# Serving the expert group with four passes fourth instead of third in the last layer of a decoder trunk

## The chip, the core and the metric

The kernel runs on one core of a Trainium2 chip. The metric is the device time of one execution in microseconds (us), lower is better. Five engines work side by side and wait for one another by semaphores: PE (matrix products, with PEld for its weight loads), DVE (vector), ACT (scalar), POOL (not used in the part treated here) and SP, which here only issues the DMAs that bring weights from the device memory (HBM) into the on-chip memory.

## What is computed

The reference is a decoder trunk of two layers over 256 tokens of width 1024. Each layer is a mixer of four kinds of attention heads, a cross-attention into 256 memory tokens, and a mixture of experts; each of the three is followed by a residual sum and a layer norm. The change concerns the order of work in the mixture of experts of the second (last) layer:

```python
def one_sequence(xs):
    g_logits = (xs @ w_group + b_group)
    g_idx = argmax(g_logits)                       # one group of 8 for each token
    g_weight = take_along_axis(softmax(g_logits), g_idx)
    e_logits = (xs @ w_expert + b_expert).reshape(s, 8, 4)[arange(s), g_idx]
    top_val, top_idx = top_k(e_logits, 2)          # two experts of 4 in that group
    top_w = softmax(top_val) * g_weight
    ...
    hid = silu(xs @ w_gate[e]) * (xs @ w_up[e])    # 1024 -> 256, twice
    return sum over e of (hid * gates[:, e]) @ w_down[e]   # 256 -> 1024
```

Each of the 32 experts has three matrices of 1 MB (gate, up, down), so a group of four experts has twelve tiles of 1 MB. How many tokens an expert gets is known only when the router has run.

## The kernel before, in words

The mixture of experts is the function `moe`. It serves the eight groups one after the other in the order of the table `SERVED[l]`: in the last layer 1, 3, 0, 2, 4, 5, 6, 7. For one group, the function `expert` runs a pass over up to 32 tokens of each of the four experts at once: the four experts take a quarter of PE's columns each. A pass is made of

- `up_to` with the four gate tiles (64 matmuls, L1277), a silu on ACT, then `up_to` with the four up tiles (64 matmuls, L1277); between the two stand the last four matmuls (L1322) of the previous group, put off as `late_back`;
- the gather of the next group's tokens (`gather_half`, 32 matmuls, L1227), and the transposition of the hidden values (`turned`, L1290);
- a branch (`over`, L1368) that is taken into further passes when an expert of the group has more than 32 tokens, more than 64 and so on, and that otherwise jumps over their code, which stands in the program behind it;
- the down product (`down`: 32 matmuls at L1306, then L1322 back to token order), with `begin` for the next group on DVE in between.

A light group has one pass. With these inputs, group 2 has a second pass, run whole before its own down product, and group 0 has three further passes. Group 0 stands in the table `SPREAD`: its three further passes run their first halves (`part`, function `hidden`) one behind the other, and their down halves (`rest`) afterwards, so that its gate and up tiles are given back between the two.

The weights come through a plan, one list of tiles in the order in which they are served. `feed` gives the next tile of the list a buffer as soon as one is free, and `done` frees a tile's buffer: the eight gate and up tiles of a group behind its branch (`free(g, 0, 8)`), its four down tiles behind its down product (`free(g, 8, 12)`). There are 21 such buffers in the last layer (six called main, nine ext, two in M, and R, VM, KT and xx), so a tile is loaded into the buffer of the tile 21 places ahead of it in the list. The loads are issued by SP in the order of the list, save that some small ones of the last group go early. The first 21 tiles of the last layer are loaded before its router has run, whether needed or not (L270); the rest are issued when the counts are known, each inside `tc.If`, so that an expert without tokens costs no load (L275). Two experts of group 6 have no tokens.

The up and down tiles of group 7 are loaded in pieces of 512 KB and 256 KB, and its down product runs over 512 columns first and then twice over 256, so that little is left to do when the last piece has landed.

Of the kernel before, what the change touches and what calls it, by code (L numbers as in the profile page):

```python
# [30 lines left out]
KEYS = 4  # L31


SERVED = [(0, 1, 2, 3, 4, 5, 6, 7), (1, 3, 0, 2, 4, 5, 6, 7)]
SPREAD = [(), (0,)]
TELL = [(3, 6), (3, 8)]


FIRST = [o[0] for o in SERVED]
GNUM = [[f if g == 0 else 0 if g == f else g for g in range(8)] for f in FIRST]  # L40
# [130 lines left out]
def trunk(ctx, tc, a, out, dbg=None, depth=DEPTH):  # L171
# [10 lines left out]
    def one(pool, name, shape, dt=F32):  # L182
        return tiles(pool, name, 1, shape, dt)[0]
# [27 lines left out]
    def square(l, m, q):  # L211
        wsq_i[l][m][q] = item(a["wsq"][l, m, q])
# [11 lines left out]
    for l in range(depth):  # L224
# [5 lines left out]
        for m in (3, 4):  # L230
            for q in range(4):
                square(l, m, q)
        for g, h in [(g, h) for g in SERVED[l + 1 == depth] for h in range(3)]:
            ids = exp_i[l].setdefault(g, {})
# [859 lines left out]
    def moe(l, pz, pb):  # L1094
# [3 lines left out]
        ff = one(pz, "ff", [128, 2, D])  # L1098
        served, spread = SERVED[late], SPREAD[late]
        follow = dict(zip(served, served[1:]))  # L1100
# [507 lines left out]
```

## Time and profile before

| | |
|---|---|
| median of 3 runs | 1008.36 us (1008.21 to 1008.63) |
| profiled execution | 1013.67 us, of which the span of the profile is 1011.9 us |
| busy: PE, PEld, DVE, ACT | 923.1, 688.2, 503.3, 340.9 us |
| DMA | 272.59 MB, mean 269 GB/s |

The span runs from the first to the last profiled instruction of the program. In the rows further below, a window is a stretch of the span (from:to) and its length in us, then the busy time and the count of PE, PEld, DVE, ACT and POOL, the clock granted to PE (1.00 is its higher level of 2.4 GHz, 0.50 its lower one of 1.2 GHz), the mean busy share of the DMA engines and the GB/s that they moved; a window of one line has only the engines that run it. A row of a timeline has the start, the duration, engine, line, operation, the tiles written and read, the count, and in brackets the idle time ahead of it with what ended that. A row that stands for several instructions has the duration of the whole run of them. Busy time is a mean over stages of different kinds: the mixture of experts of the last layer fills the last quarter of the span, from 757.81 us on, and only its stages matter for this change.

### The profile page before, as it was taken

What the parts mean: (1) busy time and instruction counts of PE and PEld (TensorE: products, weight loads), DVE (VectorE), ACT (ScalarE), POOL (GpSimd) and SP (SyncE); (2) the same over time, 40 slices, a digit from 0 to 9 for tenths busy, and PEclk for the clock granted to TensorE, in tenths of its full rate; (3) what the DMA queues carried; (4) which work ended last, traced back from release to release, by engine and by line L of the source; (5) the groups of instructions that cost most, each with busy time, mean ns of one, the idle gap of its engine ahead of it and who ended that gap; (6) DMA issues with size and microseconds to landing.
All of it is one profiled execution on the core that took longest, in us unless ns stands there. A gap on an engine that the chain in (4) does not pass through costs nothing. (4 is left out here: it accounts for less than half of the span.)

```text
span 1011.9 us, 19936 instructions
## 1 busy us (share of the span) xinstructions
PE 923.1 (91%) x7948; PEld 688.2 (68%) x7948; DVE 503.3 (50%) x1258; ACT 340.9 (34%) x736; POOL 0.2 (0%) x4
## 2 busy tenths in 40 slices
PE   7899999999998688989899999999999888997885
PEld 7888987898754354856368899789885564444541
DVE  5755755544653333323466575554465414644434
ACT  5454855343411121011144475435442121121111
POOL 0000000000000000000000000000000000000000
PEclk9999999999999899999999999999999999999998
DMA  9842334538769988999786244553784994719995
GB/s 351 343 147 99 134 128 161 209 125 331 293 268 422 424 348 367 424 425 420 250 336 229 108 147 180 174 208 110 288 351 196 421 387 183 318 58 421 422 363 203
DMA packets 43774, 272.59 MB, mean 269 GB/s; under 512 B 4832, under 2 KB 5344, under 8 KB 13280
## 3 DMA queue, kind: packets, MB, share of 16 engines
q1 hardware_dynamic: 43472, 270.26, 68.2%
q8 instruction: 86, 1.41, 0.5%
q14 instruction: 72, 0.59, 0.2%
q10 hardware_dynamic: 144, 0.33, 0.1%
HBM read 269.52 MB, written 1.05 MB: 267 GB/s over the span
## 5 line engine op out<-in xcount | busy, mean ns | idle before, releaser
L432 DVE SCALAR_TENSOR_TENSOR wl<-main,wh 128x1024 fp32r<-128x1024 f32 (+1 forms) x93 | 112.2, 1211 | 112.1 <-ACT wh L431 111.9
L431 ACT ACTIVATE wh<-main 128x1024 fp32r<-128x1024 f32 (+1 forms) x93 | 97.3, 1052 | 116.5 <-PE bank L438 68.3
L437 PE MATMUL bank<-xh,wh 128*128 128x256 f32 x368 | 108.8, 298 | 5.6 <-ACT xh L488 3.6
L438 PE MATMUL bank<-xl,wh 128*128 128x256 f32 x368 | 105.8, 288 | 1.0 <-DVE xl L432 0.6
L439 PE MATMUL bank<-xh,wl 128*128 128x256 f32 x368 | 104.9, 286 | 0.0
L1277 PE MATMUL bank<-ext,xg 128*32 128x256 f32 x912 | 88.2, 392 | 2.9 <-DMA ext<-exp 2.8
L1327 DVE TENSOR_TENSOR ff<-ff,bank 128x512 f32<-128x512 f32 x84 | 53.2, 681 | 49.9 <-PE bank L1322 49.9
L437 PEld LDWEIGHTS bank<-xh,wh 128*128 128x128 f32 x368 | 71.1, 194 | 7.0 <-ACT xh L488 4.1
L438 PEld LDWEIGHTS bank<-xl,wh 128*128 128x128 f32 x368 | 71.3, 194 | 2.2 <-DVE xl L432 0.9
L439 PEld LDWEIGHTS bank<-xh,wl 128*128 128x128 f32 x368 | 71.4, 194 | 0.1
L1277 PE MATMUL bank<-main,xg 128*32 128x256 f32 x640 | 66.1, 384 | 2.4 <-DMA main<-exp 2.4
L460 ACT ACTIVATE xg<-bank,prmb 128x128 f32<-128x128 f32 x64 | 24.0, 456 | 123.3 <-PE bank L1227 117.2
L1310 ACT ACTIVATE y<-bank,sm 128x512 fp32r<-128x512 f32 (+1 forms) x46 | 30.7, 669 | 103.5 <-PE bank L1306 76.1
L1322 PE MATMUL bank<-y,dt 128*128 128x512 f32 (+1 forms) x184 | 56.9, 422 | 7.9 <-DVE y L1311 7.2
L1306 PE MATMUL bank<-ext,dn 128*32 128x512 f32 (+1 forms) x212 | 46.6, 670 | 17.5 <-PEq L1368 6.8
L437 PE MATMUL bank<-wh,oh 128*128 128x512 f32 (+1 forms) x160 | 60.9, 380 | 0.0
L439 PE MATMUL bank<-wh,ol 128*128 128x512 f32 (+1 forms) x160 | 59.1, 369 | 0.0
L1322 PEld LDWEIGHTS bank<-y,dt 128*128 128x128 f32 x184 | 29.6, 188 | 43.2 <-ACT y L1310 16.4
L438 PE MATMUL bank<-wl,oh 128*128 128x512 f32 (+1 forms) x160 | 59.0, 369 | 0.0
L1277 PEld LDWEIGHTS bank<-ext,xg 128*32 128x32 f32 x912 | 42.6, 112 | 22.5 <-issue 4.7
L1227 PEld LDWEIGHTS bank<-dn,xhat 128*128 128x128 f32 x448 | 51.1, 192 | 5.8 <-issue 4.9
L1227 PE MATMUL bank<-dn,xhat 128*128 128x128 f32 x448 | 53.7, 278 | 0.0
(300 smaller groups left out, 2008.7 us busy)
## 6 DMA issues: line engine op xcount, KB each, us to landing
ext<-exp SPq DMA_DIRECT2D x75, 1024.0 KB, 16.6
main<-exp SPq DMA_DIRECT2D x54, 1024.0 KB, 12.8
main<-wsq SPq DMA_DIRECT2D x33, 1024.0 KB, 5.0
main<-win SPq DMA_DIRECT2D x22, 1024.0 KB, 6.8
M<-exp SPq DMA_DIRECT2D x17, 1024.0 KB, 15.0
VM<-exp SPq DMA_DIRECT2D x8, 1024.0 KB, 17.1
xx<-exp SPq DMA_DIRECT2D x7, 1024.0 KB, 14.0
M<-wsq SPq DMA_DIRECT2D x5, 1024.0 KB, 7.1
```

The lines of the kernel that those rows point to most:

```text
L431: ACT.activation(hi, src, AF.Copy, scale=scale)
L432: DVE.scalar_tensor_tensor(lo, src, scale, hi.bitcast(F32), op0=ALU.mult, op1=ALU.subtract)
L437: PE.matmul(psum, lh, rh, start=first, stop=False, skip_group_check=True)
L438: PE.matmul(psum, lh, rl, start=False, stop=False, skip_group_check=True)
L439: PE.matmul(psum, ll, rh, start=False, stop=last, skip_group_check=True)
L460: ACT.activation(dst, src, AF.Identity, bias=b, scale=g)
L1227: PE.matmul(b[:, k * 128:(k + 1) * 128], xhat[:, t, c:c + 128], d[:, t], start=(t == 0 and k == 0), stop=(t == 1), skip_group_check=True)
L1277: PE.matmul(pg[m * i:m * i + m, which * S:(which + 1) * S], x[:, k, m * i:m * i + m], w[:, k], start=(k == 0), stop=(k == 7), skip_group_c ...
L1306: PE.matmul(b[m * i:m * i + m], ht[:, f * 128 + m * i:f * 128 + m * i + m], w[:, o:o + n], start=(f == 0), stop=(f == 1), skip_group_check ...
L1310: ACT.activation(hi, b, AF.Copy, scale=gate)
L1322: PE.matmul(bs[t], dt[:, t * 128:(t + 1) * 128], y[i], start=(i == 0 and not held), stop=(i == 1), skip_group_check=bool(held))
L1327: DVE.tensor_add(o, o, bs[t])
```

## The change

One line of the table changes. In the last layer the order of the groups was 1, 3, 0, 2, 4, 5, 6, 7 and becomes 1, 3, 4, 0, 5, 2, 6, 7: group 4 is served before group 0, and group 5 before group 2. The plan of loads is built from the same table, so the weights of group 4 are also loaded ahead of those of group 0, and those of group 5 ahead of those of group 2. No instruction is added or removed.

```diff
-SERVED = [(0, 1, 2, 3, 4, 5, 6, 7), (1, 3, 0, 2, 4, 5, 6, 7)]
+SERVED = [(0, 1, 2, 3, 4, 5, 6, 7), (1, 3, 4, 0, 5, 2, 6, 7)]
 SPREAD = [(), (0,)]
 TELL = [(3, 6), (3, 8)]
```

On PE, behind the first pass of the third group served, the kernel before goes on with group 0 (spread over `part`):

```order
L1227 MATMUL bank_7_68<-dn_0_13924,xhat_0_77 128x128 x8
L1290 MATMUL bank_1_62<-cst_0_70,hs_0_13922 128x128 x2
L1368 COMPARE_AND_BRANCH
L1363 REGISTER_ALU
L1604 BRANCH_PREFETCH_HINT
L1227 MATMUL bank_3_64<-f_61_0_13925,xhat_0_77 128x128 x8
L1227 MATMUL bank_5_66<-f_61_0_13925,xhat_0_77 128x128 x8
```

At the same place the changed kernel stands in group 4, and what follows the branch is the code of a second pass that its 18 tokens of the fullest expert do not need:

```order
L1227 MATMUL bank_7_68<-dn_0_13924,xhat_0_77 128x128 x8
L1290 MATMUL bank_1_62<-cst_0_70,hs_0_13922 128x128 x2
L1368 COMPARE_AND_BRANCH
L1227 MATMUL bank_3_64<-f_61_0_13925,xhat_0_77 128x128 x8
L1227 MATMUL bank_5_66<-f_61_0_13925,xhat_0_77 128x128 x8
```

The tiles, the banks and the place of the branch are the same; the group behind them is another. What stood there moves one group down: from the row at which the fifth group reads its count (row 11751 on PE) the two programs are alike row by row again, with group 5 in the changed kernel where group 4 was.

On SP the loads stand in the same order, buffer by buffer. Only the branches between them move. Before, the three-way branch of group 0's `rest` stood behind the twelfth load that follows group 0's first branch, ahead of the one into VM:

```order
L275 DMA R_0_76<-exp 128x2048
L274 UNCONDITIONAL_BRANCH x2
L1368 COMPARE_AND_BRANCH x3
L1368 UNCONDITIONAL_BRANCH x4
L274 COMPARE_AND_BRANCH
L275 DMA VM_0_75<-exp 128x2048
```

Now it stands twelve loads later, ahead of the one into main_1:

```order
L275 DMA main_5_125<-exp 128x2048
L274 UNCONDITIONAL_BRANCH x2
L1368 COMPARE_AND_BRANCH x3
L1368 UNCONDITIONAL_BRANCH x4
L274 COMPARE_AND_BRANCH
L275 DMA main_1_121<-exp 128x2048
```

So the twelve loads from VM on, which before had to wait for a buffer of group 0's down tiles or of group 2, now take the buffers of group 4's down tiles and of group 0's gate and up tiles.

## Rows read from the trace of the kernel before

**Rows 1.** The page: the span, and the chain that ended last, by engine.

```profile
span 1011.9 us, 19936 instructions
DMA 8%; DVE 1%; PE 1%; issue 0%; SPq 0%; DVEq 0%; ACT 0%
```

**Rows 2.** Windows from group to group, served 1, 3, 0, 2, 4, 5, 6, 7.

```profile
757.81:776.46 18.65, 16.94 (x207) 10.23 (x207) 12.73 (x58) 5.80 (x14) 0.00 (x0) 1.00 0.26 92
776.46:797.52 21.06, 17.41 (x204) 9.98 (x203) 8.63 (x26) 3.43 (x8) 0.00 (x0) 1.00 1.01 421
797.52:874.16 76.64, 69.22 (x809) 40.56 (x808) 32.40 (x92) 14.47 (x32) 0.00 (x0) 1.00 0.74 306
874.16:911.19 37.03, 34.59 (x406) 20.14 (x405) 16.39 (x46) 7.18 (x16) 0.00 (x0) 1.00 0.40 154
911.19:936.18 24.99, 19.78 (x204) 10.73 (x203) 9.95 (x30) 3.54 (x8) 0.00 (x0) 0.93 1.01 422
936.18:956.27 20.09, 17.33 (x204) 9.98 (x203) 8.52 (x26) 3.53 (x8) 0.00 (x0) 1.00 1.01 422
956.27:976.41 20.14, 17.34 (x204) 9.98 (x203) 9.03 (x26) 3.53 (x8) 0.00 (x0) 1.00 1.01 413
976.41:1001.38 24.97, 22.29 (x199) 9.60 (x198) 6.97 (x13) 3.69 (x6) 0.00 (x0) 1.00 0.80 283
```

**Rows 3.** Windows in which the weight stream pauses (columns as in rows 2).

```profile
834.20:847.60 13.40, 11.35 (x168) 7.60 (x160) 2.88 (x10) 1.89 (x5) 0.00 (x0) 1.00 0.01 3
886.50:905.50 19.00, 17.28 (x203) 9.77 (x201) 5.28 (x15) 5.29 (x13) 0.00 (x0) 1.00 0.01 2
```

**Rows 4.** The last group: two windows, and a PE row with its wait.

```profile
976.41:988.83 12.42, 11.48 (x133) 5.11 (x132) 2.44 (x4) 1.67 (x2) 0.00 (x0) 1.00 0.86 285
990.33:994.82 4.49, 3.99 (x16) 0.72 (x16) 0.00 (x0) 0.00 (x0) 0.00 (x0) 1.00 1.04 392
...
991.79 0.62 PE L1306 MATMUL bank<-R,dn 128*32 128x512 f32 x1 [0.34 <-DMA R<-exp]
```

**Rows 5.** Timeline of PE: a light group's second pass; windows of L1306: its down product.

```profile
781.18 3.66 PE L1277 MATMUL bank<-ext,xg 128*32 128x256 f32 x64
...
950.19:953.84 3.65, 3.64 (x32) 0.94 (x32) 1.00 1.01 415
```

**Rows 6.** Timeline of group 4's branch: PE, then PEld.

```profile
927.69 1.62 PE L1306 MATMUL bank<-ext,dn 128*32 128x512 f32 x5 [4.15 <-DMA main<-exp]
...
933.21 0.16 PEld L1306 LDWEIGHTS bank<-ext,dn 128*32 128x32 f32 x8 [2.15 <-issue]
```

**Rows 7.** Timeline of SP from the first load that waits for the counts.

```profile
771.09 3.75 SPq L275 DMA_DIRECT2D main<-exp  x6
...
789.93 15.31 SPq L275 DMA_DIRECT2D ext<-exp  x7
807.37 0.33 SPq L275 DMA_DIRECT2D xx<-exp  x1
809.79 2.77 SPq L275 DMA_DIRECT2D main<-exp  x2
```

**Rows 8.** DMA issues at 802.47 and at 812.23 alone: size, us to landing.

```profile
ext<-exp SPq DMA_DIRECT2D x1, 1024.0 KB, 19.4
main<-exp SPq DMA_DIRECT2D x1, 1024.0 KB, 19.5
```

**Rows 9.** Timeline of PE: the last tile of the third group's second pass.

```profile
802.44 0.40 PE L1277 MATMUL bank<-R,xg 128*32 128x256 f32 x1
```

**Rows 10.** Windows of PE's idle stretch in group 4, and of what followed.

```profile
923.60:927.60 4.00, 0.00 (x0) 0.00 (x0) 0.04 (x1) 1.54 (x5) 0.00 (x0) 1.00 1.01 416
928.00:931.30 3.30, 3.30 (x18) 1.03 (x12) 1.94 (x11) 0.09 (x1) 0.00 (x0) 0.50 1.01 420
```

**Rows 11.** Timeline of PE: the end of group 5.

```profile
955.61 0.73 PE L1322 MATMUL bank<-y,dt 128*128 128x512 f32 x2 [1.11 <-DVE y L1311]
```

**Rows 12.** The page: the queue that brings instructions.

```profile
q8 instruction: 86, 1.41, 0.5%
```

## The prediction

> **What bounds the kernel now.** I looked first at the chain that ended last: of the span of 1011.9 us DMA holds 8% and no other wait over 1% [rows 1], so PE's work is the bound, with the weight stream breaking in at places. Second, windows from group to group, for the places [rows 2]. A light group with no wait takes 20.1 us; group 4 takes 24.99 and group 7 24.97. In the same view the stream is full (421 GB/s, 1.01 of the DMA engines) under groups 3, 4, 5 and 6, and not full under groups 0 and 2. Third, windows of the two stretches in which it stops [rows 3]: 834.20 to 847.60, until group 0's gate and up tiles are given back, and 886.50 to 905.50, until those of group 2 are. These releases come 50.1 us (847.60 - 797.52) and 31.3 us (905.50 - 874.16) behind their group's start, since a group's further passes run with those tiles still held. What the stops lose is missed at the end. In group 7 [rows 4] the two passes up to 988.83 take 12.42 us, and the first half of its down product 4.49 (990.33 to 994.82), with a wait for a DMA inside. Without waits a pass takes 3.66 us of matmuls [rows 5], and the whole down product 3.65, so a half of it 1.8. From a group's start to its second pass group 3 needs 4.72 (781.18 - 776.46) [rows 2, 5], so both passes would be 8.4 us. So the last group waits about 4.0 + 2.7 = 6.7 us for weights.
>
> Group 4's loss is of another kind. Before its down product PE stands idle for 4.15 us, and its weight load stalls once more, 2.15 us [rows 6]. The view names a DMA of weights for the first, but the idle stands right behind PE's branch, where it jumps over the second pass. I read it as PE waiting for its next instructions, which come over a DMA queue of their own: 86 transfers, 1.41 MB [rows 12]. Behind the idle time PE runs at half clock for 3.3 us [rows 10].
>
> **The change, part by part.** No work is added, so the sum is made of waits and their places. I follow the last layer from its first changed group on.
>
> *Group 4 third.* It starts at 797.52, as group 0 did [rows 2], since groups 1 and 3 and the first 36 loads stand as before. It has one pass; with the 20.1 to 21.06 us of the light groups it ends at 817.6 to 818.6. I take 818.6, since the stream is full here as under group 3 (21.06).
>
> *Group 0 fourth: the new wait.* A load n takes the buffer of tile n-21. Up to the 45th load the list of buffers is the same and the releases too, so the landings are those of before. Now the 40th load is group 0's last gate tile and the 44th its last up tile. On SP [rows 7] 21 tiles were loaded early; then come 6 from 771.09 (22nd to 27th), seven single ones and pairs up to the 34th, 7 from 789.93 (35th to 41st), the xx one (42nd), 2 from 809.79 (43rd, 44th). The 40th is issued at 802.47 and lands 19.4 us later, at 821.9; the 44th at 812.23, 19.5 later, at 831.7 [rows 8]. The last up tile of the third group served, the 32nd, was first read at 802.44 [rows 9], and that stays so. So PE waits at group 0's first pass until 821.9, 3.3 us, runs 3.66 and the gathering beside it, and waits at the second pass until 831.7, some 5 us more. All group 0 is then late by 831.7 - 802.44 = 29.3 us against before, where the light group in front explains 21.1. So 8.2 us of the waits are lost (9.2, if that group needs 20.1).
>
> *The clock behind that wait.* Before, PE's idle 4.0 us [rows 10] was followed by a stretch at a granted clock of 0.50, the lower level, 3.30 us long. Work that takes 3.4 us there takes 1.7 at the higher one. Group 0's second wait is as long, so I charge 1.7 us. The ends: nothing, if PE's short work between the waits keeps the clock; 3.4, if each wait brings such a stretch.
>
> *Group 0 to its end.* From its last tile to its end it took 874.16 - 802.44 = 71.7 us [rows 2, 9], of which no wait is the stream's, so it ends at 831.7 + 71.7 + 1.7 = 905.1.
>
> *Group 5 fifth.* 20.09 us before [rows 2], with a wait of 1.11 for DVE at the end [rows 11], for which I read DVE's own branch under a full stream as the cause. Now loads 58 to 65 start when group 0 gives back its gate and up tiles (831.7 - 802.44 + 847.60 = 876.9, with the clock 878.6), take 8 x 2.5 us and end near 898.6; the 66th to 69th wait for its down tiles, near 904. At group 5's branch (some 9 us behind its start) the stream is thus nearly at its end, and I take half of the 1.11 away: 19.6. Ends: 19.0 and group 3's 21.06. Group 5 ends at 924.7.
>
> *Groups 2, 6, 7.* Group 2 takes its 37.03, to 961.7; group 6 its 20.1, to 981.8. Group 7 without waits is 8.4 for its passes, 1.5 as before (988.83 to 990.33) and 1.8 for half the down product: 993.5. Before, that point stood at 994.82 [rows 4]. What follows it I leave as it was.
>
> Are group 7's weights there in time? Loads 82 on wait for group 2's gate and up tiles, 31.3 us behind its start, at 956.0. From there about 10.25 MB are wanted before group 7's second pass, which starts at 924.7 + 37.0 + 20.1 + 4.7 = 986.5. At 421 GB/s [rows 2] a tile of 1 MB (1.049 million bytes) takes 2.49 us, so with 3 us until the first lands they are in at 984.5. The margin is 2 us. The Trainium skill, "DMA: Bandwidth & Descriptors", section Specifications, gives about 358 GB/s as the limit of HBM for one core; by it the same tiles would take 30.0 us instead of 25.5, the margin would be gone and the time, an estimate by that page, 2.5 us longer. The rows of this kernel hold 421 with one core at work, and I go by them.
>
> **The sum.** Gained: 6.7 at group 7 and 4.9 at group 4 (24.99 - 20.1), and about 0.5 at group 5: 12.1. Lost: 8.2 of waits at group 0, 1.7 of clock, and 1.0 for group 4's 21.06 instead of 20.1. That is -1.2; walked through, the point at 994.82 moves to 993.5, -1.3 us, which I use: the profiled execution, 1013.67 us with its span of 1011.9, would be 1012.4. It lies 5.3 above the median of 1008.36, and I put the difference on the median: **1007.1 us**.
>
> **The rivals.**
>
> *A, a clear gain.* The waits at group 0 bring no half clock (1.7) and group 5 needs only 19.0 (0.6): -3.6 us, 1004.8; with the clock alone 1005.4. For it: the waits are two, with work between; against it: the second is as long as the idle time of [rows 10]. It decides whether PE's clock falls at 831.7.
>
> *B, slower: the branch pays again.* On PE and SP the program from the fifth group on stands row for row where it stood, only with group 5 in group 4's place. If group 4's idle 4.15, its half clock and its stall [rows 6, 10] belong to that place in the program and not to the moment, group 5 takes 24.99 instead of 19.6: +5.4 - 1.3 = +4.1, 1012.5. It decides from a jump 3.4 us late on. The Trainium skill, "Runtime: NRT & Kernel Launch", section Instruction fetch mechanics, says that a taken branch whose target is not in the pages already fetched stops the engine until a DMA brings it. By that rule each jump would cost. The rows bear it out only in part: groups 5 and 6 jump over second passes too and take 20.09 and 20.14 [rows 2]. Against B: group 4 jumped under a stream at 422 GB/s that filled the queues, group 5 will jump where it is at its end. For it: the place is the same.
>
> *C, the last group waits again.* If loads 82 on start some 2 to 4 us later than worked out, the margin is eaten and up to 2 us return: 1009.2. For it: the start of group 7 still hangs on the release in group 2; against it: the stream has two stops less to make good than before, as loads 46 to 57 now run before the first.
>
> **How the numbers follow.** The forecast has 0.52, A 0.24, B 0.14, C 0.10. A measurement of this kernel tells about 0.2%, 2.0 us, from no change: the bounds are 1006.3 and 1010.4. Faster takes A and a small part of the forecast's own width (1005.9 to 1008.4, from group 5's and the clock's ends): 0.3. Slower takes B: 0.14. The rest, 0.56, is within. The range goes from A's end, 1004.8, up past C to 1010.6, and leaves out most of B and what lies under A.
>
> **What would show it.** In the profile of after: PE's waits for DMA ahead of group 0's two passes, ending near 821.9 and 831.7, and a granted clock of 0.50 behind the second; group 0's end near 905; starts of groups 2, 6 and 7 near 925, 962 and 982; no wait for a DMA in group 7; stops of the stream near 863 to 879 and 941 to 956. At group 5's branch, PE idle under 2 us shows B wrong, one of 4 us shows it right. The forecast falls if the 40th and 44th load land at other times, since each us there is a us at the end until group 7's margin, or if group 7's passes still take 12 us.

## The result: 0.55% slower

The changed kernel takes 1015.04 us (median of 10 runs) where the kernel before takes 1008.58 in as many runs: ratio 1.0055, interval 1.0036 to 1.0073, so about 5.5 us slower (the two medians lie 6.5 apart). The forecast was 1007.1, 1.3 us faster, and the time lies outside its range.

The page of the changed kernel, for [rows 1]: the span, and the chain that ended last, by engine.

```profile
span 1013.4 us, 19936 instructions
DVE 1%; PE 0%; issue 0%; ACT 0%; DVEq 0%
```

The 8% of DMA are gone from the chain: the chain that ends the changed kernel holds no wait for weights any more. Windows from group to group, served 1, 3, 4, 0, 5, 2, 6, 7 (columns as in rows 2; the last one ends, as there, with the last matmul):

```profile
755.49:774.15 18.66, 16.95 (x208) 10.24 (x207) 12.75 (x58) 5.80 (x14) 0.00 (x0) 1.00 0.27 94
774.15:794.29 20.14, 17.34 (x203) 9.98 (x202) 8.62 (x26) 3.53 (x8) 0.00 (x0) 1.00 1.01 421
794.29:815.61 21.32, 17.90 (x203) 10.28 (x202) 9.06 (x28) 3.53 (x8) 0.00 (x0) 1.00 1.01 422
815.61:903.10 87.49, 74.11 (x809) 41.51 (x808) 32.42 (x92) 14.47 (x32) 0.00 (x0) 0.96 0.76 314
903.10:923.90 20.80, 17.67 (x204) 10.14 (x203) 9.62 (x30) 3.54 (x8) 0.00 (x0) 1.00 0.76 301
923.90:962.65 38.75, 34.66 (x406) 20.16 (x405) 15.93 (x44) 7.18 (x16) 0.00 (x0) 1.00 0.56 219
962.65:984.36 21.71, 19.02 (x204) 10.68 (x203) 9.02 (x26) 3.54 (x8) 0.00 (x0) 0.92 1.02 400
984.36:1002.86 18.50, 17.06 (x199) 8.89 (x198) 6.99 (x13) 3.68 (x6) 0.00 (x0) 1.00 0.58 219
```

The layer starts 2.3 us earlier here than before (755.49 against 757.81), which has nothing to do with the change, so I count from group 1's first matmul. Up to the point that the forecast walked to, the end of the first half of the last down product (994.82 before, [rows 4]; 996.29 here), the kernel before takes 237.0 us and the changed one 240.8; the forecast was 235.7. Group 0 is 10.9 us longer than in [rows 2] and ends at 147.6 (903.10 - 755.49), where the forecast said 147.3. Everything behind it was to take 88.4 us and takes 93.2.

The timeline of PE at group 0's start, for [rows 9]:

```profile
816.76 0.62 PE L1277 MATMUL bank<-ext,xg 128*32 128x256 f32 x2 [0.53 <-DMA ext<-exp]
819.20 0.62 PE L1277 MATMUL bank<-ext,xg 128*32 128x256 f32 x2 [1.82 <-DMA ext<-exp]
821.64 6.14 PE L1277 MATMUL bank<-ext,xg 128*32 128x256 f32 x58 [1.82 <-DMA ext<-exp]
...
831.39 0.40 PE L1277 MATMUL bank<-main,xg 128*32 128x256 f32 x1 [1.81 <-DMA main<-exp]
```

The issues of the 40th and the 44th load alone, at 800.16 and 809.95, for [rows 8]:

```profile
ext<-exp SPq DMA_DIRECT2D x1, 1024.0 KB, 21.4
main<-exp SPq DMA_DIRECT2D x1, 1024.0 KB, 21.4
```

Windows of the two stretches at half clock between the layer's first group and its last matmul, one in this wait, one behind group 2 (for [rows 10]):

```profile
820.00:826.70 6.70, 5.06 (x48) 2.37 (x52) 0.00 (x0) 0.00 (x0) 0.00 (x0) 0.50 1.01 428
963.30:966.60 3.30, 3.30 (x36) 1.74 (x32) 1.65 (x3) 0.00 (x0) 0.00 (x0) 0.50 1.03 355
```

The wait is there as forecast: PE waits tile by tile in the first pass, and for the last up tile in the second. On the time scale of this run the forecast's ends are 819.6 and 829.4; both come 2.0 us later. The two loads are issued when the forecast said, and take 21.4 us to land instead of 19.4 and 19.5. The half clock (0.50, the level of 1.2 GHz) lies inside the wait: the first pass runs slowly while the next tiles are still to come, and nothing in group 0 is at half clock behind 831.39.

Behind group 0 the time goes in small pieces at the branches over unused passes. The timeline of PE in group 2's down product:

```profile
961.98 0.73 PE L1322 MATMUL bank<-y,dt 128*128 128x512 f32 x2 [1.85 <-DVE y L1311]
```

DVE comes late, as I read it because its own branch was late (the kernels with shifted code below bear that out); the idle time is followed by the second stretch at half clock, which makes group 6 1.6 us longer.

### The profile page after: what moved, and what is told of

Same layout as the page of the kernel before. It is cut to its first block, busy times and chain, and to the rows that moved or that the text cites. A ratio compares the mean times of both kernels' runs of the same rounds, so it can differ in the third digit from the quotient of the medians.

```text
span 1013.4 us, 19936 instructions
## 1 busy us (share of the span) xinstructions
PE 920.5 (91%) x7948; PEld 687.5 (68%) x7948; DVE 503.0 (50%) x1258; ACT 340.9 (34%) x736; POOL 0.2 (0%) x4
## 5 line engine op out<-in xcount | busy, mean ns | idle before, releaser
L1277 PE MATMUL bank<-ext,xg 128*32 128x256 f32 x912 | 92.9, 403 | 7.5 <-DMA ext<-exp 7.5
L1277 PE MATMUL bank<-main,xg 128*32 128x256 f32 x640 | 63.9, 381 | 3.6 <-DMA main<-exp 3.6
L1310 ACT ACTIVATE y<-bank,sm 128x512 fp32r<-128x512 f32 (+1 forms) x46 | 30.8, 669 | 96.3 <-PE bank L1306 71.7
L1306 PE MATMUL bank<-ext,dn 128*32 128x512 f32 (+1 forms) x212 | 43.4, 623 | 16.5 <-PEq L1368 5.5
## 6 DMA issues: line engine op xcount, KB each, us to landing
VM<-exp SPq DMA_DIRECT2D x8, 1024.0 KB, 19.6
```

The costliest lines, as they stand in the source:

```text
L1277: PE.matmul(pg[m * i:m * i + m, which * S:(which + 1) * S], x[:, k, m * i:m * i + m], w[:, k], start=(k == 0), stop=(k == 7), skip_group_c ...
L1306: PE.matmul(b[m * i:m * i + m], ht[:, f * 128 + m * i:f * 128 + m * i + m], w[:, o:o + n], start=(f == 0), stop=(f == 1), skip_group_check ...
L1310: ACT.activation(hi, b, AF.Copy, scale=gate)
```

## The experiments

**Theory 1**, in its first form: the forecast's walk holds up to group 0's end, and the loss behind it is what the branches cost there, by their place in the program. **Theory 2** is the rival named with each run: chance of one execution, the order itself, or the clock. Where a time "to L1345" is given, it runs from group 1's first matmul to the matmul that follows the first half of the last down product, in the profiled execution. All ratios are against the kernel before, run on the same chip beside it.

**Each kernel once more** (no edit).

> The kernel before, unchanged, in a second profiled execution. Theory 1 (the loss of the change lies behind group 0, at jumps over unused passes and what follows them): the weight stream runs without a pause from 905.5 us on in the trace of before, so its last layer takes 237.0 us from group 1's first matmul (757.81) to L1345 (994.82) again, within 1 us, whether or not group 4's idle time of 4.15 us comes back, since the stream hides it. Theory 2 (the profiled execution of before was an unlucky sample, its own time being 5.3 us above the median): the same stretch takes 3 to 5 us less.

Measured: 236.1 us to L1345, as theory 1 said. Group 4's branch is there again, in the timeline of PE:

```profile
924.06 1.60 PE L1306 MATMUL bank<-ext,dn 128*32 128x512 f32 x8 [4.19 <-DMA main<-exp]
```

> The changed kernel, unchanged, in a second profiled execution. First profile: 240.8 us from group 1's first matmul to L1345, with losses of 1.2 us in group 5, 1.7 in group 2 and 1.6 in group 6 against the forecast. Theory 1: these three come back at the same places within 1 us each, and 240.8 comes back within 1.5 us. Theory 2 (chance of one execution): they are elsewhere or gone, and the stretch lies between 236 and 245.

Measured: 242.7 us to L1345; groups 5, 2, 6 and 7 take 20.27, 39.06, 20.02 and 15.75 (to L1345). The wait at the end of group 2 came back to the hundredth, group 6's half clock did not, and PE stood idle for 3.19 us at group 7's branch, which it hadn't in the first profile. So theory 1 held at two of its three places, and 242.7 lies 1.9 us above 240.8, outside its 1.5:

```profile
958.78 0.74 PE L1322 MATMUL bank<-y,dt 128*128 128x512 f32 x2 [1.85 <-DVE y L1311]
...
992.09 1.03 PE L1306 MATMUL bank<-ext,dn 128*32 128x512 f32 x1 [3.19 <-PEq L1368]
```

"PEq L1368" says it plainly: PE's own sequencer was at the branch. Group 4's branch in the one kernel and group 2's wait in the other thus come back with the program, while what stands at group 7 depends on the moment as well. The profiled execution of before was no unlucky sample of this layer.

**Without the branches of the six light groups** (both orders; the code of further passes, the branch over it and the hint that PE gets ahead of the branch are left out where these counts need none):

```diff
-                with apart():
-                    over(full[g], part if wide else whole, label=label[0])
+                if not late or g in (0, 2):
+                    with apart():
+                        over(full[g], part if wide else whole, label=label[0])
```

> The changed kernel with the code of further passes, and so the branch over it, left out in the last layer for the six groups that have one pass with these inputs (1, 3, 4, 5, 6, 7). Theory 1: nothing is gained up to group 0's second pass, where PE waits for a weight tile that lands as before (831.3); behind it the waits at the jumps of groups 5 and 6 (3.1 and 2.7 us) go, so the time falls by 5 to 8 us against the changed kernel, to about the kernel before or up to 2.5 us under it. Theory 2 (the jumps cost nothing that matters): within 2 us of the changed kernel, 5 us above before.

Measured: ratio 0.9969 (0.9946 to 0.9993), 233.9 us to L1345.

> The kernel before with the same code left out for groups 1, 3, 4, 5, 6, 7 of the last layer. Theory 1: the time stays within 1.5 us of before, though every such jump has 1.65 us or more of PE idle time in the trace, because the landing of group 0's last up tile (802.4) and the stream without a pause from 905.5 set its end. Theory 2 (PE's own waits set the end): 4.9 us at group 4 and 1.65 at each of groups 1, 3, 5 and 6 come off, 8 to 11 us faster than before.

Measured: ratio 0.9935 (0.9913 to 0.9958), 229.8 us to L1345. For before theory 1 is wrong: the branches are paid there too, and 6.5 us come off, between its 1.5 and theory 2's 8 to 11. For the changed kernel its size is about right, but by luck: of the 6.9 us between the two profiles (240.8 to 233.9) 5.0 come ahead of group 0's end (142.6 instead of 147.6), where it expected nothing, and 1.9 behind it, where PE now stands idle for 3.67 us at group 2's branch. The stream is not as fixed as I had it: without group 1's branch SP issues its first load at 759.15 instead of 771.09 [rows 7] (layer start 755.48 against 757.81), and the 44th load lands 7 to 9 us earlier in both orders (66.5 and 66.7 us behind the start, 73.9 and 75.9 with the branches).

**Without any branch** (group 0's three further passes and group 2's one stand as plain code, the others are left out, in both orders):

```diff
+                more = {0: 3, 2: 1}.get(g, 0) if late else None
...
-                    over(full[g], part if wide else whole, label=label[0])
+                    if more is None:
+                        over(full[g], part if wide else whole, label=label[0])
+                    else:
+                        for c in range(1, more + 1):
+                            (part if wide else whole)(c, lambda: None)
...
-                    over(full[g], rest, top=3)
+                    for c in range(1, 4):
+                        rest(c, lambda: None)
```

> The changed kernel without any branch over passes in the last layer: the three further passes of group 0 and the one of group 2 stand in the program as plain code, the others are left out (right for these counts alone). Theory 1 (the forecast's walk holds, the loss behind group 0 is what jumps cost there): from group 1's first matmul to L1345 the walk gives 56.1 to group 0, its last up tile at 66.8 as without the light groups' jumps, 71 us to its end at 138, then 18.7, 37.0, 18.7 and 11.7: 224 to 227 us, against 240.8 and 242.7 with jumps; about 6 to 10 us faster than the kernel before it is compared with. Theory 2 (something else in the order costs those 5 us, the weights or the clock): 229 us or more.

Measured: ratio 0.9817 (0.9784 to 0.9851), 221.3 us to L1345, faster than either theory said. Windows of groups 0, 5, 2, 6 and 7:

```profile
810.76:890.62 79.86, 73.00 (x809) 41.52 (x808) 32.92 (x91) 14.50 (x32) 0.00 (x0) 0.96 0.77 322
890.62:909.35 18.73, 17.08 (x203) 10.06 (x203) 7.94 (x22) 3.54 (x8) 0.00 (x0) 1.00 0.98 410
909.35:945.43 36.08, 34.24 (x405) 20.03 (x404) 17.37 (x50) 7.20 (x16) 0.00 (x0) 1.00 0.75 298
945.43:964.15 18.72, 17.07 (x203) 10.06 (x203) 7.13 (x18) 3.54 (x8) 0.00 (x0) 1.00 1.02 386
964.15:975.98 11.83, 10.68 (x151) 5.25 (x150) 3.43 (x6) 2.05 (x3) 0.00 (x0) 1.00 0.41 145
```

> The kernel before without any branch over passes in the last layer, in the same way. Theory 1: its end is set by the weight stream behind group 2's release, so it stays near what it is without the light groups' jumps (229.8 us to L1345): 227 to 230, slower by 1 to 5 us than the changed order without branches, the other way round than with them. Theory 2: it stays faster than the changed order, by the 4 to 5 us that the two profiles of each show.

Measured: ratio 0.9763 (0.9732 to 0.9795), 213.2 us to L1345. Windows of groups 0, 2 and 7:

```profile
792.69:864.42 71.73, 68.58 (x809) 40.27 (x808) 32.02 (x85) 14.51 (x32) 0.00 (x0) 1.00 0.71 294
864.42:900.50 36.08, 34.25 (x405) 20.04 (x404) 19.23 (x59) 7.20 (x16) 0.00 (x0) 1.00 0.71 290
...
956.66:968.49 11.83, 10.68 (x151) 5.24 (x150) 3.43 (x6) 2.05 (x3) 0.00 (x0) 1.00 1.03 387
```

Here theory 1 fell: no turn of the sign. Without branches neither order waits for weights at its end (11.83 us in group 7 in both), and the two differ in one row, group 0: 79.86 against 71.73, with PE's clock at 0.96 in the one and 1.00 in the other. These 8.1 us are the new wait and the half clock, which here outlasts it: the last up tile is first read at 821.26, and the clock is at 0.50 until 826.1, which costs some 2.4 of the 8.1. Nothing pays for them. In the times of the runs the two orders lie 6 us apart (medians of 992.29 and 986.24), the sign and about the size that theory 2 gave. The forecast's gain at group 7 exists only where branches have held up the stream.

One row more from this profile is needed to read the others, the timeline of PE ahead of group 4's down product:

```profile
914.51 0.64 PE L1306 MATMUL bank<-ext,dn 128*32 128x512 f32 x4 [1.65 <-ACT dn L427]
```

PE stands idle there for 1.65 us without any branch, since it waits for ACT. So of the 4.15 us of [rows 6] only 2.5 are the branch's, and an idle time of 1.65 us at a branch is none of its cost.

**The two halves of the change** (all branches kept):

```diff
-SERVED = [(0, 1, 2, 3, 4, 5, 6, 7), (1, 3, 0, 2, 4, 5, 6, 7)]
+SERVED = [(0, 1, 2, 3, 4, 5, 6, 7), (1, 3, 0, 5, 2, 4, 6, 7)]   # only5
+SERVED = [(0, 1, 2, 3, 4, 5, 6, 7), (1, 3, 4, 0, 2, 5, 6, 7)]   # only4
```

> One half of the change alone: group 5 between the two long groups, group 0 third as before (1, 3, 0, 5, 2, 4, 6, 7), all branches kept. Theory 1: no wait at group 0 (its end at 116.4 as before), and the stream gets ahead, so the end is set by PE: 116.4 + 20.4 + 38.9 + 20 to 25 + 20.1 + 11.7 = 227.5 to 232.5 to L1345, 4 to 9 us faster than before. Theory 2 (a light group behind group 0 costs by itself): 237 or more.

Measured: ratio 0.9914 (0.9883 to 0.9944), 225.5 us to L1345, faster than both kernels, and 2 us under the range of theory 1, whose 4 to 9 us hold in the times of the runs (0.86%, 8.7 us). Windows of groups 0, 5, 2 and of the last (to L1345):

```profile
791.30:868.89 77.59, 69.65 (x810) 40.30 (x809) 32.42 (x92) 14.47 (x32) 0.00 (x0) 1.00 0.75 308
868.89:887.60 18.71, 17.06 (x204) 10.07 (x203) 9.68 (x30) 3.53 (x8) 0.00 (x0) 1.00 0.79 313
887.60:924.61 37.01, 34.82 (x405) 20.28 (x404) 15.96 (x44) 7.18 (x16) 0.00 (x0) 1.00 0.83 339
...
965.18:977.96 12.78, 10.87 (x152) 5.68 (x151) 2.87 (x5) 2.05 (x3) 0.00 (x0) 1.00 0.91 308
```

> The other half alone: group 4 ahead of group 0, groups 2 and 5 in their old order behind it (1, 3, 4, 0, 2, 5, 6, 7), all branches kept. Theory 1: group 0 ends at 147.5 as in the changed kernel, since it waits for the same landings; then 37.0 to 38.9 + 20 to 21 + 20.1 + 11.7 to 15: 236.5 to 243, no faster than before (0 to +6 us). Theory 2 (group 5's place is what costs): 232 to 236, some 3 us faster than before.

Measured: ratio 1.0072 (1.0044 to 1.0100), 247.7 us to L1345. Group 0 ends at 147.55, as theory 1 said to the tenth; the tail is worse than it said (236.5 to 243), with 3.60 us of idle time at a branch in group 2 and 3.24 in group 7. Putting a light group ahead of group 0 is the half that costs, putting one behind it the half that gains: group 0 waits for nothing new, and the weights get ahead while group 5 runs.

**The place of the code.** 64 matrix instructions and/or 64 vector instructions that never run, in a pass of group 1 that its 4 tokens jump over, push PE's or DVE's later program down:

```diff
                 def whole(c, hint):
+                    if late and g == first and c == 1:
+                        b = banks.get()
+                        for _ in range(64):
+                            PE.transpose(b[:, 0:128], hs[0][:, 0:128], ident)
+                        banks.put(b)
+                        k = tiny(4).rearrange("p (t j) -> p t j", t=2)
+                        for _ in range(64):
+                            DVE.tensor_scalar(k, keyg[:, g], 0.0, None, op0=ALU.add)
```

(In the one for a single engine the other loop runs once.)

> The changed kernel with 64 more matrix instructions (with their weight loads) that never run: they stand in the second pass of group 1 in the last layer, which its 4 tokens jump over, so that PE's whole program behind them stands 64 matmuls and 64 weight loads further down. Theory 1 (what a jump costs depends on where its code and its target lie among the pieces in which the program is fetched): PE's branches behind, which took 4.7 us in group 4, 3.8 in group 5 and 2.2 to 3.4 in groups 6 and 7, take other times, by a microsecond or more in two of them, and the time to L1345 changes by more than 1.5 us, either way; DVE's late branch in group 2 (PE idle 1.86) stays. Theory 2 (the costs come from the moment, the load on the DMA engines): each as before within 0.7 us, and the time is the changed kernel's, 5 us above before.

Measured: ratio 1.0071 (1.0046 to 1.0096), 244.4 us to L1345. Group 4's branch went from 2.94 us of idle time to 4.17, group 5's from 1.98 to 1.65, which is what PE waits there anyway, and group 2's wait for DVE stayed (1.85). One branch changed by more than a microsecond against both profiles of the changed kernel, where theory 1 wanted two, and the ratio moved by less than its interval.

> The changed kernel with 64 more vector instructions that never run, in the same place, so that only DVE's program behind stands lower. Theory 1: PE's branches keep their times within 0.7 us; the wait of PE for DVE at the end of group 2 (1.86 and 1.85 us in two profiles) goes or moves to another group. Theory 2: it stays, and the time is the changed kernel's.

Measured: ratio 1.0043 (1.0026 to 1.0061), 242.0 us. Group 2's wait for DVE is gone (37.04 us instead of 38.75 and 39.06); group 1 became 1.2 us longer and group 3 1.4 shorter. PE's branch in group 4 kept its time (2.64 us of idle time, 2.94 and 2.62 without the padding), as theory 1 said.

> The changed kernel with both sets of instructions that never run. Theory 1: the branch times of the kernel with the matrix instructions alone, and group 2's end as in the one with the vector instructions alone. Theory 2: all as in the changed kernel.

Measured: ratio 1.0044 (1.0019 to 1.0068), 241.5 us. Group 2's end is as theory 1 said (37.0 us); the branch times are not: group 4's is down to 1.65 us of idle time, group 7's up to 5.38, where the kernel with the matrix instructions alone had 4.17 and 3.35. PE's code stands in the same place in these two, so this place alone does not set what a branch costs.

> The kernel before with the 64 matrix instructions that never run. Theory 1: group 4's branch, 5.9 and 6.0 us in two profiles with PE idle for 4.15 and 4.19, comes down by 2 us or more, with no half clock behind it; others may rise. As the weight stream without a pause from 905.5 on hides what group 4 loses, the time to L1345 moves by less than 3 us. Theory 2: group 4's branch keeps its 5.9 us.

Measured: ratio 1.0041 (1.0023 to 1.0059), 240.7 us. The long branch moved from group 4 to group 5 with its size unchanged, and group 7 got one as well. The timeline of PE, these two:

```profile
943.96 1.03 PE L1306 MATMUL bank<-main,dn 128*32 128x512 f32 x1 [4.15 <-PEq L1368]
...
987.77 1.03 PE L1306 MATMUL bank<-ext,dn 128*32 128x512 f32 x1 [3.38 <-PEq L1368]
```

So code that never runs makes the kernel before almost as slow as the change does. Theory 1 is right that the stall moves with the code; its bound of 3 us on the end was too small.

What PE waits for in such a stall can be seen in the trace. The DMA queues in group 4's idle stretch of before (923.54 to 927.69), then in the same group here, where PE stands idle for 1.65 us (917.96 to 919.62), the rows of the instruction queues (transfers, MB, share of the 16 DMA engines' time):

```profile
q8 instruction: 1, 0.02, 1.5%
q14 instruction: 2, 0.02, 0.9%
...
q14 instruction: 1, 0.01, 1.2%
```

A transfer of 16 KB on q8 lies in the long stretch and none in the short one. The same holds through all profiles: in the last layer PE stands idle for 2.6 us or more ahead of a down product in 25 places, and in each a transfer on q8 starts inside the stretch, or up to 0.2 us ahead of it, and PE goes on 1.7 to 2.1 us behind its end. So the reading of the stall as a wait for instructions is borne out.

**Is the 0.55% place or order?** The kernel before, and the half that gained, in more places:

> The kernel before with the 64 vector instructions that never run. Theory 1 (place is a cost of its own on top of the order): PE's branches as before, 5.9 us in group 4 among them, DVE's late branches at other groups; 0 to 0.4% slower. Theory 2 (the kernel before had a lucky place, and the order costs nothing): 0.4 to 0.7% slower, like the changed kernel in its four places (0.43 to 0.71%).

Measured: ratio 0.9997 (0.9977 to 1.0017), 237.4 us to L1345, as theory 1 said; group 4's idle time 4.24 us.

> The kernel before with both sets of instructions that never run. Theory 1: 0 to 0.4% slower than before, less than the changed kernel with both sets (0.44%). Theory 2: 0.4 to 0.7%.

Measured: ratio 1.0017 (0.9995 to 1.0039), 239.8 us, theory 1 again; long branches in group 5 (4.23 us) and group 7 (3.69).

> Group 5 alone moved (1, 3, 0, 5, 2, 4, 6, 7), with the 64 matrix instructions that never run. Both theories: the order's gain is the weight stream's (the last group no longer waits), so a part of the 0.86% stays: 0.2 to 0.9% faster than before. If it is all place: 0.2% faster to 0.4% slower.

Measured: ratio 0.9948 (0.9922 to 0.9975), 233.6 us.

> The same order with both sets of instructions that never run: 0.2 to 0.9% faster than before; if its gain was place, 0.2% faster to 0.4% slower.

Measured: ratio 0.9988 (0.9967 to 1.0010), 236.2 us, in the range for place; 5.69 us in group 7's branch.

In the same place the changed order is slower than the order before every time: by 0.55% with no padding, 0.30 (1.0071 - 1.0041), 0.46 and 0.27 with the three, 0.4% in the mean. Of these the 0.30 and the 0.27 are by themselves not clear of the two intervals that each is made of. A change of place alone makes up to 0.4% in the kernel before and up to 0.7% in the order with group 5 moved alone, whose gain is real in two places of three and not shown in the third.

**Only the branches of the tail taken away** (those of the one-pass groups behind group 0 in the one order, shown here, and behind group 2 in the other, with (1, 3, 0, 2) in place of the list):

```diff
-                with apart():
-                    over(full[g], part if wide else whole, label=label[0])
+                if not late or g in (1, 3, 4, 0, 2):
+                    with apart():
+                        over(full[g], part if wide else whole, label=label[0])
```

> The changed kernel with the code of further passes and the branch over it left out only for the groups with one pass behind group 0 in the last layer (5, 6 and 7). Theory 1 (behind group 0 the changed kernel is bound by PE, so every branch counts): from group 0's end (147.5) the rest takes 85.5 to 90 us instead of 93.2 and 95.1, about what the forecast gave (88.4); 233 to 238 to L1345, 4 to 9 us faster than the changed kernel. Group 2's own branch stays, and its place moves, so up to 4 us of that may not come. Theory 2 (the stream or the clock holds the rest back): 240 or more.

Measured: ratio 0.9992 (0.9971 to 1.0012), 237.5 us to L1345; the part behind group 0 takes 86.7 us, as theory 1 said. The forecast's walk had 88.4 there, of which some 2.3 are what its lengths of groups 5 and 6 (19.6 and 20.1) lie above 18.7, what such a group takes without its branch; without them it is 86.1. Group 0, whose code is as in the changed kernel, took 88.3 us here and ended at 150.8: a stretch at half clock fell behind its last up tile (first read at 827.65):

```profile
828.00:831.30 3.30, 3.30 (x40) 1.58 (x36) 0.00 (x0) 0.00 (x0) 0.00 (x0) 0.50 1.02 429
```

> The kernel before with the same left out only for groups 4, 5, 6 and 7, all behind group 2. Theory 1 (the weight stream, which runs without a pause from group 2's release on, sets the end and hides branches): 235 to 238 to L1345 against 237.0 and 236.1, the waits for weights in group 7 growing by what the groups ahead save; within 2 us of before. Theory 2 (the branches are paid there too): 4.9 us at group 4 and 1 to 2 at each of groups 5 and 6 come off, 228 to 232.

Measured: ratio 0.9931 (0.9907 to 0.9955), 232.5 us to L1345. Theory 1 missed again: the groups 4, 5 and 6 save 6.1 us, and group 7, which was to wait for weights by as much longer, takes 19.0 instead of 18.4. Windows of groups 4, 5, 6 and 7 (to L1345):

```profile
904.07:922.78 18.71, 17.06 (x203) 10.05 (x202) 11.93 (x43) 3.53 (x8) 0.00 (x0) 1.00 1.01 419
922.78:944.09 21.31, 18.37 (x204) 10.80 (x203) 7.41 (x18) 3.53 (x8) 0.00 (x0) 1.00 1.01 426
944.09:963.18 19.09, 17.44 (x203) 11.05 (x203) 6.49 (x14) 3.54 (x8) 0.00 (x0) 1.00 1.02 426
963.18:982.22 19.04, 15.54 (x151) 6.12 (x150) 3.41 (x6) 2.05 (x3) 0.00 (x0) 1.00 1.03 402
```

The last row is the one to compare with the last of [rows 2]: 402 GB/s here, 283 and a share of 0.80 there (312 and 0.90 if it too ends at L1345, 976.41:994.82). Under group 7 the kernel before does not run its stream at full rate, which that row said and I passed over. Without the branches it does, and the weights are in earlier.

## Why the prediction was wrong

The branch-free order of before (213.2 us) gives a floor for each group; what lies above it, in us, is the mean of the two profiles of each kernel:

| group | 3 | 4 | 0 | 5 | 2 | 6 | 7 | sum |
|---|---|---|---|---|---|---|---|---|
| before | 1.8 | 6.2 | 5.5 | 1.4 | 0.9 | 1.3 | 6.3 | 23.4 |
| changed | 1.4 | 3.1 | 15.3 | 1.8 | 2.8 | 2.2 | 2.0 | 28.6 |
| difference | -0.4 | -3.1 | +9.8 | +0.4 | +1.9 | +0.9 | -4.3 | +5.2 |
| forecast | 0 | -3.9 | +9.9 | -0.5 | 0 | 0 | -6.7 | -1.2 |

(A floor is 18.7 for a light group, 71.7 for group 0, 36.1 for group 2, 11.8 for group 7 up to L1345; as an example, group 7 in the changed kernel: the mean of 11.93 and 15.75, less 11.83, is 2.0.)

- **Group 0's new wait: right in size, in part by luck.** 8.2 us of waits and 1.7 of clock were forecast, 9.8 in all came. The make-up differs, and two errors cancel: the tiles landed 2.0 us later than worked out, and the half clock cost nothing, because it fell inside the wait. The second is a matter of the execution: in a_tail 3.4 us of half clock lay behind the last up tile, and from there to its end group 0 took 73.9 us instead of 71.7, 2.2 more, where the forecast charged 1.7. The step "landings are those of before" was off by the 2.0 us, in both profiles. Up to the 36th load the landings are those of before (54.4 us behind the layer's start in both); the 37th and the 38th then land 3.4 us behind the load ahead of them instead of 2.4, beside group 4's branch, for which five transfers run on the instruction queues between 52 and 60 us, where before there is one. Without any branch the 44th load lands alike in both orders (66.6 and 67.0 us). So the 2.0 us go with the branches; that these transfers hold up the tiles is likely and not shown.
- **The failed step: groups 5, 2, 6 and 7 walked through at 19.6, 37.0, 20.1 and 11.7 us, with no price for their branches beyond what stood in the rows of before.** I had read group 4's 24.99 us as a loss that the change takes away (4.9 us in the sum). It went there, but branches cost elsewhere in its stead. In the kernel before the long stall stood in group 4 (4.15, 4.19, and 4.24 with vector padding) or, with matrix padding, in group 5 (4.15, 4.23) with another in group 7; in the changed kernel small pieces stand in several groups, and a long one in group 7 in four of five profiles (3.2 to 5.4 us). The four lengths came out 0.9, 1.9, 0.8 and 2.1 us longer in the mean of the two profiles, 5.7 us in all, nearly the whole gap between -1.2 and +5.2. a_tail, which takes three of the branches away, shows the walk itself right: 86.7 us, and 86.1 in the walk without them.
- **Rival B had the mechanism and the wrong place.** It let group 5's branch cost what group 4's had cost, since the program stands there row for row. PE's idle time at group 5's was 1.65 to 1.98 us, of which 1.65 are no branch's, and groups 2, 6 and 7 paid. So the same place on PE cost 2.5 us above the 1.65 in one order and next to nothing in the other: where a branch stands on PE is not all that counts. DVE's program, whose places the rows of PE don't tell, was not looked at.
- **The gain at group 7 is a gain only against a kernel with branches.** It came, smaller (4.3 us instead of 6.7), because group 7's branch took its place. Without branches there is none, and the change costs its wait and the half clock: 8.1 us in the profiles.
- **The margin of 2 us for group 7's weights held.** No wait for weights stands in group 7 in either profile of the changed kernel, so rival C and the lower HBM rate that the Trainium skill gives ("DMA: Bandwidth & Descriptors", Specifications) played no part; 422 GB/s was reached under group 4 and 400 under group 6.
- **Rival A is out.** It hung on whether the clock falls at the last landing. It had fallen before, at 819.9, and was back at 826.7, so the half clock cost nothing, as A wanted, and yet no gain came.

The rule of the Trainium skill that I set against the rows ("Runtime: NRT & Kernel Launch", Instruction fetch mechanics: a taken branch to code that is not in the pages at hand waits for a DMA) is borne out better than I weighed it: I took groups 5 and 6 at 20.1 us for groups whose branches cost nothing, and they lie 1.4 us above 18.7, most of it a wait for DVE at their end (1.11 in [rows 11]). The trace agrees: PE goes on when a transfer on q8 is over, in all 25 long stalls. That a shift of code that never runs moves the 4.2 us from one group to another is what this rule could make; which branch then pays is not settled by PE's place alone, as group 5 and the two paddings with matrix instructions show.

**Open:** why one branch waits for a transfer on q8 and the next does not; and why the weight stream of before slackens under group 7 and not in b_tail. Two of its tiles land 3.4 us apart there (970.8, 974.2, 977.6) instead of 2.4, as beside group 4's branch in the changed kernel, and group 6's branch stands in that stretch, but no run took that branch alone away. What of a place's cost belongs to PE and what to DVE was shown for groups 4, 5 and 2, not for all.

## What to carry to other kernels

A stall at a taken branch moves when the code shifts and when the order changes, so a forecast may not book it as gained when groups change places. Give the branches of the new path a price, from nothing up to the worst of the old ones, and measure an order in two or three places (some instructions that never run suffice) before believing a difference under 0.5%. A light stage between two long ones helps where the weights get ahead during it and the next stage's tiles are already in, as group 5 behind group 0; ahead of the first long stage it only moves that stage's tiles back in the queue. And read the share of the DMA engines in every window: a stage that waits for weights while that share is 0.80 or 0.90 is not bound by the rate alone.

## What the runs showed of the hardware that was not expected

- Code that never runs cost 0.41% of the kernel before, 64 matmuls with their weight loads in a pass that is jumped over; 64 vector instructions there cost nothing (0.9997), and both 0.17%, which is not clear of noise.
- In all 25 stalls of 2.6 us and more at a down product PE went on 1.7 to 2.1 us behind the end of a 16 KB transfer on the instruction queue q8, also where the profile puts the wait down to a DMA of weights.
- The branches of one layer, with their hints and the unused code behind them, cost some 23 us out of 1009: the order before without any takes 986.24 us. Its groups lose the 23.4 us of the table, in waits at the branches and at what they hold up. SP alone started its loads some 10 us later with the branch of the first group (759.15 against 771.09 us, starts 2.3 us apart).
- The half clock at a wait need not cost: in the changed kernel 6.8 us of it lay inside the wait for the next tiles. In a_straight 4.8 us of such a stretch outlasted the wait, and in a_tail one of 3.4 us began behind it.
